# The end of even attention: one gated group finished apart, a bias as a product, and the heads first into the output projection

## The chip, the cores and the metric

The kernel runs on one core of one Trainium2 chip. The metric is the device time of one execution in microseconds (us); several runs are taken and their median is compared. The engines are named as in the profile: PE (matrix products), PEld (its weight loads), DVE (vector), ACT (activations and copies), POOL (a second elementwise engine), SP (which issues the DMAs).

## The reference

Two layers, each a mixer and a feed-forward network, over 512 tokens and 256 context tokens with 1024 channels, in fp32. The change lies in the mixer of the even layer. Its input projection gives u and v for a gated MLP over chunks of 128 tokens, and q, k and values for four heads of differential attention; both results, side by side, go through one output projection.

```python
def chunk_mlp(u, v, w_s, b_s):             # 4 groups of 128 channels
    u = gelu(u).reshape(shp)               # shp = (b, t // 128, 128, 4, 128)
    vf = gelu(v).reshape(shp)
    mu = mean(vf, axis=-1)
    vf = (vf - mu) * rsqrt(mean((vf - mu)**2, axis=-1) + EPS)
    mixed = einsum('gpq,bnqgc->bnpgc', w_s, vf) + b_s.T[None, None, :, :, None]
    return (u * mixed).reshape(b, t, A_WIDTH)

def diff_out(o, g, lam_init):              # o: attention's result by head
    return (rmsnorm(o, g) * (1.0 - lam_init)).reshape(b, t, B_V_WIDTH)

# even mixer, and the same for the context tokens with hc:
y = concatenate([chunk_mlp(u, v, w_s, b_s), diff_out(o, subln_g, lam_init)], -1) @ w_out
```

## The kernel before, in words

Activations lie with 128 channels on the partitions and all 768 tokens (512 and 256 context) along the row, so a tile of 128x768 is one group of channels. An fp32 product is made of three products of fp32r halves: `split` gives a tile's high half by a cast on ACT (L115) and its low half by a subtraction on DVE or POOL (L116), and `mm3` issues high by high (L99), high by low (L100) and low by high (L101). Weights are loaded by SP into a ring (`unit`, tile raw), cast on ACT (L75) and their low half is made on POOL (L78); the result is called w.

A tile framework sets the order of the instructions of each engine when the program is built, by the order in which they are written, by priorities, and by `issue_after`, which keeps an instruction behind a named one in that order and adds no wait of its own. The engines then run their queues in that order, each instruction waiting for its operands and for its buffers. PSUM has three short buffers (`bank`, tiles pb), one fill buffer (`fill`, tiles pf) and two wide ones (`wide`, pw).

The end of the even mixer's attention consists of these steps:

- `head(t)`: attention of a head, in three blocks of 256 queries. Its result o is normed by `norm`: squares on ACT (L592), sums over the channels on PE (L150), on DVE the mean (L159) and a root by three Newton steps (L129 to L133) on 128x6 numbers, six diagonal tiles q (L166), a product that spreads them over the partitions (L176), and the multiplication (L600). The root is written as one instruction for a start value and nine for the steps.
- `gated(i)`: 24 products of 512 and 24 of 256 columns into the fill buffer, copied to a tile f on ACT (L576). Groups 4 to 7 are v, groups 0 to 3 are u.
- `turn(g)`: group g of v is turned by PE (L635), copied back on ACT (L636), and its mean and variance are taken on DVE (L639, L640).
- then one `rstd_small` for all 24 columns of the four groups, and for each g `mix(g)`: normalising on DVE (L649), product with the chunk matrix sguT on PE (L650), the bias sgub added on DVE from a tile in which it is repeated on all partitions (L651).
- the cat loop: for u's groups the gelu on ACT (L623) and the gate product on DVE (L678), for all eight tiles the split into halves (tiles ax). The low halves of heads 5 and 6 are made on POOL.
- `project(half, ...)`: the output projection with the slabs of `even_out`, in the order of the list `order`, in two halves of the tokens, 192 products of 384 columns each. Between the casts of slabs on ACT stands the silu of the next stage's modulation with its table load (L206).

The two lines on which the ring's work depends are

```python
nc.scalar.copy(hi, raw)                                   # L75
eng.tensor_tensor(lo, raw, hi.bitcast(F32), ALU.subtract) # L78
```

## Time and profile before

| what | value |
|---|---|
| median of 3 runs | 1641.04 us (1639.45 to 1643.92) |
| profiled execution | 1640.6 us, its span 1638.8 us, mean granted clock 0.979 |
| PE busy | 1539.0 us, 94% of the span |
| DVE, ACT, POOL busy | 1098.8, 724.7, 650.6 us |
| chain that ended last | PE 79%, DVE 10%, ACT 4% |

The stretch that the change rewrites begins at 303.97 us of the span, with the first product of gated group 2, and its last part, the first half of the output projection, ends at 379.85. Rows of the timeline give the start, the duration, the engine, the line, the operation, out<-in and, in brackets, the idle time of that engine ahead of it with what ended it; "x8" are eight instructions in a row of one kind. The share of PEclk is the TensorE clock that the chip granted, 1.00 being full speed.

### The profile page before, as it was taken

To read this page: it belongs to the slowest core of one execution; us is meant where nothing else is said; L and a number is where in the kernel's file an instruction comes from. 1 tells how busy PE (TensorE), PEld (TensorE's weight loads), DVE (VectorE), ACT (ScalarE), POOL (GpSimd) and SP (SyncE) were. 2 spreads that over 40 slices of the span, in tenths; PEclk is the share of its full clock that TensorE was granted. 3 is DMA by queue.
4 is the path that set the end of the run, shared out by engine and by line. 5 is a ranking of instruction groups with operands and counts; after the bars stand their busy time and mean duration, and the time that the engine had idled before them with its cause. 6 is when DMAs were issued, how large, how long until landed. Compare 5 with 4: busy or idle time off the path is not lost.

```text
span 1638.8 us, 24612 instructions
## 1 busy us (share of the span) xinstructions
PE 1539.0 (94%) x9463; PEld 1352.8 (83%) x9463; DVE 1098.8 (67%) x2097; ACT 724.7 (44%) x1464; POOL 650.6 (40%) x477
## 2 busy tenths in 40 slices
PE   6999989989889999999999999999998799999997
PEld 4776777889678988999999978776867699999996
DVE  4621787755786888766667485675667876676565
ACT  2423675543452333333333344465555545444443
POOL 0563111050573334343333415531304665554563
PEclk9999989999999999999999999999999799999999
DMA  8744100123132234434432102100213232332311
GB/s 318 299 164 158 40 7 1 47 83 129 39 116 90 97 136 137 146 130 153 136 122 77 63 26 78 60 32 14 71 72 110 78 129 85 109 116 78 116 40 52
DMA packets 47957, 161.97 MB, mean 99 GB/s; under 512 B 5472, under 2 KB 9952, under 8 KB 40160
## 3 DMA queue, kind: packets, MB, share of 16 engines
q1 hardware_dynamic: 47696, 160.28, 28.0%
q8 instruction: 74, 1.21, 0.3%
q14 instruction: 43, 0.35, 0.1%
q10 hardware_dynamic: 144, 0.13, 0.1%
HBM read 158.29 MB, written 2.10 MB: 98 GB/s over the span
## 4 chain that ended last, share of the span: by engine, by line
PE 79%; DVE 10%; ACT 4%; issue 3%; POOL 2%; DMA 1%; SPq 0%; POOLq 0%; DVEq 0%; ACTq 0%
PE pw L99 10%; PE pw L100 10%; PE pw L101 10%; PE pb L100 9%; PE pb L101 9%; PE pb L99 9%; PE pf L99 3%; PE pf L100 3%; PE pf L101 3%; PE pb L1199 2%; PE pb L1193 2%; PE pf L350 2%; PE pw L1157 1%; PE pw L1165 1%; DVE hh L874 1%
## 5 line engine op out<-in xcount | busy, mean ns | idle before, releaser
L904 POOL TENSOR_TENSOR w<-raw,w 128x512 fp32r<-128x512 f32 x126 | 184.2, 1470 | 141.5 <-ACT w L902 132.7
L78 POOL TENSOR_TENSOR w<-raw,w 128x512 fp32r<-128x512 f32 (+1 forms) x84 | 125.7, 1504 | 232.6 <-ACT w L75 207.4
L99 PE MATMUL pw<-ax,w 128*128 128x384 f32 (+2 forms) x640 | 206.1, 326 | 6.7 <-ACT hs L969 4.1
L100 PE MATMUL pw<-ax,w 128*128 128x384 f32 (+2 forms) x640 | 207.8, 325 | 2.4 <-DVE ax L457 1.4
L101 PE MATMUL pw<-ax,w 128*128 128x384 f32 (+2 forms) x640 | 205.5, 324 | 0.0
L904 POOL TENSOR_TENSOR w<-rawo,w 128x512 fp32r<-128x512 f32 x80 | 114.1, 1427 | 214.7 <-ACT w L902 205.6
L758 DVE SCALAR_TENSOR_TENSOR xT<-pb,mod,xT 128x512 f32<-128x512 f32 (+3 forms) x208 | 144.9, 705 | 66.0 <-PE pb L101 65.4
L100 PE MATMUL pb<-hh,w 128*128 128x512 f32 x480 | 170.9, 358 | 1.9 <-POOL hh L116 1.9
L99 PE MATMUL pw<-T,w 128*128 128x384 f32 (+1 forms) x504 | 158.5, 317 | 13.0 <-ACT T L115 6.6
L902 ACT CAST w<-pf 128x512 fp32r<-128x512 f32 x152 | 89.4, 588 | 181.4 <-DVE pf L926 59.7
L101 PE MATMUL pb<-hh,w 128*128 128x512 f32 x480 | 168.6, 358 | 0.0
L99 PE MATMUL pb<-hh,w 128*128 128x512 f32 x480 | 164.9, 358 | 3.8 <-ACT hh L115 3.8
L100 PE MATMUL pw<-T,w 128*128 128x384 f32 (+1 forms) x504 | 158.5, 315 | 3.7 <-POOL T L116 2.4
L101 PE MATMUL pw<-T,w 128*128 128x384 f32 (+1 forms) x504 | 157.9, 313 | 0.0
L99 PEld LDWEIGHTS pw<-ax,w 128*128 128x128 f32 x640 | 122.8, 193 | 16.0 <-ACT hs L969 6.1
L904 DVE TENSOR_TENSOR w<-pf,w 128x512 fp32r<-128x512 f32 x152 | 104.2, 686 | 41.6 <-ACT w L902 37.5
L100 PEld LDWEIGHTS pw<-ax,w 128*128 128x128 f32 x640 | 123.3, 193 | 10.2 <-DVE ax L194 2.6
L101 PEld LDWEIGHTS pw<-ax,w 128*128 128x128 f32 x640 | 123.4, 193 | 3.4 <-POOL w L904 0.2
L99 PEld LDWEIGHTS pw<-T,w 128*128 128x128 f32 x504 | 97.0, 193 | 18.9 <-ACT T L115 8.6
L99 PE MATMUL pb<-ax,w 128*128 128x256 f32 (+1 forms) x340 | 104.0, 308 | 2.8 <-ACT w L75 1.6
L902 ACT CAST w<-raw 128x512 fp32r<-128x512 f32 x126 | 76.6, 622 | 63.8 <-PE pw L101 62.2
L100 PE MATMUL pb<-ax,w 128*128 128x256 f32 (+1 forms) x340 | 103.9, 306 | 1.0 <-DVE ax L116 0.9
(398 smaller groups left out, 4041.1 us busy)
## 6 DMA issues: line engine op xcount, KB each, us to landing
raw<-ffn_in SPq DMA_DIRECT2D x44, 1024.0 KB, 6.2
ar<-ada SPq DMA_DIRECT2D x24, 1024.0 KB, 7.1
ar<-ada SPq DMA_DIRECT2D x48, 512.0 KB, 3.5
rawo<-ffn_out SPq DMA_DIRECT2D x44, 512.0 KB, 3.8
raw<-odd_out SPq DMA_DIRECT2D x32, 256.0 KB, 2.7
raw<-qk SPq DMA_DIRECT2D x16, 256.0 KB, 7.9
raw<-uv SPq DMA_DIRECT2D x16, 256.0 KB, 2.8
raw<-even_out SPq DMA_DIRECT2D x8, 512.0 KB, 3.7
```

The costliest lines, as they stand in the source:

```text
L78: eng.tensor_tensor(lo, raw, hi.bitcast(F32), ALU.subtract)
L99: mm(out, s[0], m[0], start=start, stop=False, **kw)
L100: mm(out, s[0], m[1], start=False, stop=False, **kw)
L101: mm(out, s[1], m[0], start=False, stop=stop, **kw)
L350: nc.tensor.matmul(ps[32 * q:32 * q + 32, :w], cst[:, k, :], t[:, w * q:w * q + w], start=k == 0, stop=k == KT - 1, skip_group_check=True)
L758: self.nc.vector.scalar_tensor_tensor(h, ps[:, r], self.modcol(l, j, m, who), h, ALU.mult, ALU.add)
L874: sub = lambda out, x, y, how: nc.vector.tensor_tensor(out, x, y, how)
L902: nc.scalar.copy(t[:, 0, :], src)
L904: (eng or nc.gpsimd).tensor_tensor(t[:, 1, :], src, t[:, 0, :].bitcast(F32), ALU.subtract)
L1157: nc.tensor.matmul(ps[:, st:en], Q, K[g][p][:, b0 * P:b1 * P], start=p == 0, stop=p == 1, skip_group_check=True)
L1193: nc.tensor.transpose(pt[:, x * P:(x + 1) * P], es[2 * (x % 2) + x // 2][:, kb * P:(kb + 1) * P], self.ident)
L1199: nc.tensor.matmul(po[64 * h:64 * h + 64, :], V[vb][:, 64 * g:64 * g + 64], t[:, h * TC:h * TC + TC], start=kb == 0, stop=kb == nb - 1, sk ...
```

## The change

It has four parts.

- The root of v's variance is taken in two pieces, `finish(0, 3)` for 18 columns behind `gated(2)`, and `finish(3, 4)` for the last 6 behind the last head's diagonals. Each piece does its gelu and its mixing; mixing of groups 0 to 2 uses the fill buffer, that of group 3 the short ones.
- The bias is a product of two rows: ones2 (2x128) by brow, which holds the high and the low half of sgub. It starts the PSUM sum to which the mixing products add. The gate product then reads u and that sum, in two pieces per group.
- The fifth product step of `gated(3)` is ordered behind the last norm's sums.
- The four heads come first in `order`, and all low halves of the cat tiles are made on DVE.

```diff
@@ rstd_diag
-                nc.tensor.matmul(ps[:, c], acc[:, c], self.ones, start=j == 0, stop=not more, skip_group_check=True)
+                self.last_sum = nc.tensor.matmul(ps[:, c], acc[:, c], self.ones, start=j == 0, stop=not more,
+                                                 skip_group_check=True)
@@ loads
-            sgub = self.load(Rv, a["sgub"].partition_broadcast(P), [P, 512], "sgub")
+            brow = Rv.tile([2, 512], F32R, name="brow")
+            sgub = self.tmp("t")[0:2, :]
+            nc.sync.dma_start(sgub, a["sgub"].partition_broadcast(2))
@@ gated
-                self.dense(ps, W, A)
+                for k in range(KT):
+                    with tc.issue_after(self.last_sum.ins) if i == 3 and off == 0 and k == 4 else ExitStack():
+                        self.mm3(ps, W[k], A[k], k == 0, k == KT - 1)
@@ mix, finish
-        def mix(g, rs):
+        ones2 = Rv.tile([2, P], F32R, name="ones2")
+        nc.vector.tensor_copy(ones2, self.ones[0:2, :])
+        bhi = self.tmp()[0:2, :].bitcast(F32R)
+        nc.scalar.copy(bhi, sgub)
+        nc.vector.tensor_tensor(brow, sgub, bhi.bitcast(F32), ALU.subtract)
+        nc.scalar.copy(brow[0:1, :], bhi[0:1, :].bitcast(F32))
+
+        def mix(g, rs, o, bank):
...
-                pw = self.fill()
+                pw = bank()
+                nc.tensor.matmul(pw[:, :n * P].rearrange("p (n q) -> p n q", q=P), ones2,
+                                 brow[:, g * P:(g + 1) * P].unsqueeze(1).to_broadcast([2, n, P]), start=True, stop=False,
+                                 skip_group_check=True)
...
-                nc.vector.tensor_tensor(vg[...], pw[...], sgub[...], ALU.add)
+                nc.vector.tensor_tensor(raw[g][:, c], raw[g][:, c], pw[:, :n * P], ALU.mult)
+
+        def finish(g0, g1, bank):
+
+            rs = self.rstd_small(mv[:, 6 * g0:6 * g1, 1], 6 * (g1 - g0), 1.0, "sf")
+            for g in range(g0, g1):
+                self.last_gelu = gelu(g, self.last_exp)
+                mix(g, rs, 6 * g0, bank)
@@ even mixer, its end
         for g in range(4):
             turn(g)
             gated(g)
-        rs = self.rstd_small(mv[:, :, 1], 24, 1.0, "sf")
-        for g in range(4):
-            mix(g, rs)
+            if g == 2:
+                finish(0, 3, self.fill)
+        with tc.issue_after(self.last_diag.ins):
+            finish(3, 4, self.bank)
+        lastg = self.last_gelu
         cat = {}
-        order = [4, 5, 6, 0, 1, 2, 3, 7]
+        order = [4, 5, 6, 7, 0, 1, 2, 3]
         for k in order:
-            if k < 4:
-                lastg = gelu(k, self.last_exp)
-                nc.vector.tensor_tensor(raw[k], raw[k], raw[4 + k], ALU.mult)
-            src = raw[k] if k < 4 else oraw[k - 4]
             cat[k] = self.ax()
-            self.split(*cat[k], src, nc.gpsimd if k in (5, 6) else nc.vector)
+            self.split(*cat[k], raw[k] if k < 4 else oraw[k - 4])
```

Lines shift in the changed kernel: the transposes are L640, the statistics L644 and L645, the normalising L664, the mixing product L666, the bias product L659, the gate product L669, the diagonals L167, the spread L177, gated's copy L581, the gelu L628, the silu L207. In the rows below, out<-in are the program's names with the number of the tile.

On PE, ahead of gated group 3 (the first L99 row here is its first product; the sums L150, the transposes L640 and the spread L177 belong to the last head's norm and to group 3 of v), the changed kernel has:

```order
L666 MATMUL pf_3082<-sguT_1295,f_361_1980 128x128 x2
L659 MATMUL pf_3090<-brow,ones_1320 128x512
L666 MATMUL pf_3090<-sguT_1295,f_368_2043 128x128 x4
L150 MATMUL pb_2746<-ones,sq_2743 128x128 x4
L150 MATMUL pb_2752<-ones,sq_2743 128x128 x2
L659 MATMUL pf_3101<-brow,ones_1320 128x256
L666 MATMUL pf_3101<-sguT_1295,f_368_2043 128x128 x2
L640 MATMUL pf_3108<-ident_97,f_375_2106 128x128 x4
L640 MATMUL pf_3122<-ident_97,f_375_2106 128x128 x2
L177 MATMUL pb_2776<-q_2768,ones 128x512
L177 MATMUL pb_2779<-q_2773,ones 128x256
L99 MATMUL pf_3141<-ax_308,w_3132 128x512
```

Here one row is left out ahead of the last one (the bias product of group 3). Before, the transposes and the statistics of all groups stood ahead of gated 3, the norm's sums in its middle, and the mixing products and the spread behind it:

```order
L650 MATMUL pf_3129<-sguT_1295,f_353_1910 128x128 x4
L650 MATMUL pf_3139<-sguT_1295,f_353_1910 128x128 x2
L650 MATMUL pf_3145<-sguT_1295,f_360_1973 128x128 x4
L99 MATMUL pw_3312<-ax_3193,w_3256 128x384
L100 MATMUL pw_3312<-ax_3194,w_3256 128x384
L99 MATMUL pw_3313<-ax_3193,w_3256 128x384
L100 MATMUL pw_3313<-ax_3194,w_3256 128x384
L176 MATMUL pb_2769<-q_2761,ones 128x512
L176 MATMUL pb_2772<-q_2766,ones 128x256
```

Mixing of groups 0 to 2, the norm and group 3's transposes moved from behind or inside gated 3 to ahead of it; behind gated 3's last product (f is filled from pf_3167) stands at once the projection's first, L99 pw with w_3281.

On DVE, the last head's norm in the changed kernel (sm and its pb are the root's numbers, pf_3108 is the first half of group 3's transposes, q are the diagonals) reads:

```order
L669 TENSOR_TENSOR f_573_2984<-f_573_2984,pf_3101 128x256
L132 TENSOR_TENSOR sm_2757<-sm_2757,pb_2752 128x6
L133 SCALAR_TENSOR_TENSOR pb_2752<-sm_2757,pb_2752 128x6
L131 SCALAR_TENSOR_TENSOR sm_2757<-sm_2745,pb_2752 128x6
L132 TENSOR_TENSOR sm_2757<-sm_2757,pb_2752 128x6
L133 SCALAR_TENSOR_TENSOR pb_2752<-sm_2757,pb_2752 128x6
L131 SCALAR_TENSOR_TENSOR sm_2757<-sm_2745,pb_2752 128x6
L132 TENSOR_TENSOR sm_2757<-sm_2757,pb_2752 128x6
L644 BN_STATS stats<-pf_3108 128x6 x3
L133 SCALAR_TENSOR_TENSOR sm_2756<-sm_2757,pb_2752 128x6
L644 BN_STATS stats<-pf_3108 128x6
L167 TENSOR_SCALAR q_2768<-ident_97,sm_2756 128x128 x4
```

One row, three aggregates (L645), is left out ahead of the last. Between the root's steps stand the last mixing product and group 3's statistics, where before the bias additions L651 and the whole gate product L678 stood.

On ACT at the end of gated 3 (o are the heads' results, f_581 and f_591 the tiles of u's group 3, w the weights of the output projection) before:

```order
L115 CAST ax_3201<-o_2156 128x768
L576 COPY f_581_3062<-pf_3089 128x256
L623 ACTIVATE f_581_3062<-f_581_3062 128x768
L75 CAST w_3256<-raw_3257 128x1024
L75 CAST w_3255<-raw_3261 128x1024
```

and in the changed kernel:

```order
L115 CAST ax_3234<-o_2163 128x768
L581 COPY f_591_3140<-pf_3167 128x256
L115 CAST ax_3238<-o_2463 128x768
L628 ACTIVATE f_591_3140<-f_591_3140 128x768
L115 CAST ax_3242<-f_555_2814 128x768
L75 CAST w_3281<-raw_3282 128x1024
L115 CAST ax_3246<-f_564_2899 128x768
L75 CAST w_3280<-raw_3286 128x1024
```

The casts of head 7 and of u's groups 0 and 1 came in between the copy of gated 3 and the casts of the first weights. On POOL the two low halves (L116) ahead of the weights' low halves are gone, and on SP the sixth to eighth slab of even_out stand behind the loads of xT and ctxT.

10 lines of the change are left out of this document (5 added, 5 removed).

## The prediction

> **What bounds the kernel now.** I read the engines' busy time first: PE works 1539.0 of 1638.8 us, so only a stretch in which it stands is worth a change. The waits of PE in the stretch that the change rewrites (from the first product of gated group 2 to the end of the first half of the output projection) come next, longest first, and the same stretch cut by what PE does. After the times of a stretch, the columns give its length, the busy time of PE, its weight loads, DVE, ACT and POOL (instructions in brackets), then the granted clock, the DMA share and GB/s.
>
> ```profile
> PE 1539.0 (94%) x9463; PEld 1352.8 (83%) x9463; DVE 1098.8 (67%) x2097; ACT 724.7 (44%) x1464; POOL 650.6 (40%) x477
> ```
>
> ```profile
> PE pb L176 <- DVE q L166: 3.8, 1, 3.8
> ```
>
> ```profile
> 303.97:379.85 75.88, 69.27 (x405) 63.66 (x404) 44.96 (x119) 30.58 (x43) 23.68 (x10) 0.96 0.33 113
> 303.97:320.90 16.93, 15.92 (x101) 13.41 (x100) 9.57 (x40) 8.72 (x16) 0.00 (x0) 1.00 0.00 0
> 320.90:330.83 9.93, 9.93 (x60) 8.74 (x60) 9.48 (x41) 4.11 (x6) 0.88 (x1) 1.00 0.78 266
> 330.83:340.17 9.34, 3.74 (x26) 3.04 (x25) 7.82 (x17) 5.98 (x7) 8.61 (x4) 0.91 0.16 56
> 340.17:345.12 4.95, 4.95 (x11) 3.74 (x12) 3.02 (x6) 4.07 (x5) 2.70 (x2) 0.50 0.32 106
> 345.12:379.85 34.73, 34.73 (x210) 34.73 (x210) 15.07 (x18) 7.71 (x10) 11.49 (x5) 1.00 0.42 141
> ```
>
> The reader is to see three things. Gated group 3 (second cut) runs without a gap, and so does the projection from 345.12 on. In the third cut PE stands for 9.34 - 3.74 = 5.6 us, 3.84 of them in one wait for the last head's norm. In the fourth it is busy all the time, but at half clock. So all that can be won here is the idle time, 75.88 - 69.27 = 6.61 us, and the loss to the clock, 4.95 / 2 = 2.48: together 9.09 us. The rows of the third cut say who holds PE: mixing's matmuls (L650) and DVE's bias additions (L651) take turns, and the gate product (L678) stands on DVE ahead of the norm's diagonals (L166).
>
> ```profile
> 334.46 1.16 PE L650 MATMUL pf<-sguT,f 128*128 128x128 f32 x8 [0.52 <-DVE f L651]
> 340.17 2.93 PE L176 MATMUL pb<-q,ones 128*128 128x512 f32 x4 [3.84 <-DVE q L166]
> ...
> 332.49 0.69 DVE L651 TENSOR_TENSOR f<-pf,sgub 128x512 f32<-128x512 f32 x1 [1.17 <-PE pf L650]
> 334.44 2.79 DVE L678 TENSOR_TENSOR f<-f,f 128x768 f32<-128x768 f32 x1
> 337.34 3.17 DVE L166 TENSOR_SCALAR q<-ident,sm 128x128 f32<-128x128 f32 x6
> ```
>
> The clock fell inside that gap. Windows of 3.41 us that end where the clock changes, here and at a second gap (464.68 on):
>
> ```profile
> 334.88:338.29 3.41, 1.44 (x11) 1.13 (x9) 3.38 (x3) 1.01 (x2) 3.41 (x2) 1.00 0.21 64
> 338.29:341.70 3.41, 1.53 (x2) 0.84 (x3) 3.41 (x8) 3.40 (x4) 1.15 (x1) 0.52 0.56 195
> 341.70:345.12 3.42, 3.42 (x10) 2.91 (x9) 1.50 (x3) 2.54 (x3) 2.70 (x2) 0.50 0.12 49
> 464.68:468.09 3.41, 2.00 (x12) 1.68 (x10) 3.41 (x4) 1.33 (x3) 3.41 (x3) 1.00 0.58 191
> 468.09:471.51 3.42, 0.58 (x3) 0.58 (x4) 3.42 (x6) 2.00 (x5) 2.38 (x3) 1.00 0.67 231
> 471.51:474.92 3.41, 3.41 (x13) 3.41 (x12) 3.23 (x4) 1.62 (x4) 2.57 (x2) 0.50 0.83 281
> ```
>
> After a window with 1.44 or 0.58 us of work the next is at half clock; after one with 2.00 it is not; and a window at half clock with 1.53 of work is followed by another.
>
> **The change, part by part.** Its durations come from these rows, beside those above:
>
> ```profile
> 321.21 0.39 PE L100 MATMUL pf<-ax,w 128*128 128x512 f32 x1
> 321.44 0.40 PE L101 MATMUL pf<-ax,w 128*128 128x512 f32 x1
> 326.47 1.50 PE L150 MATMUL pb<-ones,sq 128*128 128x128 f32 x12
> 327.73 0.36 PE L99 MATMUL pf<-ax,w 128*128 128x256 f32 x1
> 327.93 0.28 PE L100 MATMUL pf<-ax,w 128*128 128x256 f32 x1
> 328.05 0.28 PE L101 MATMUL pf<-ax,w 128*128 128x256 f32 x1
> ...
> 306.12 0.17 DVE L133 SCALAR_TENSOR_TENSOR pb<-sm,pb 128x6 f32<-128x6 f32 x1
> 306.32 0.16 DVE L131 SCALAR_TENSOR_TENSOR sm<-sm,pb 128x6 f32<-128x6 f32 x1
> 306.91 1.27 DVE L166 TENSOR_SCALAR q<-ident,sm 128x128 f32<-128x128 f32 x6
> 318.44 0.89 DVE L639 BATCH_NORM_STATS2 stats<-pf 128x6 f32<-128x128 f32 x4 [0.57 <-ACT f L636]
> 323.40 6.25 DVE L649 TENSOR_SCALAR f<-f,mv,sf 128x128 f32<-128x128 f32 x24
> ...
> 328.25 2.30 ACT L115 CAST ax<-o 128x768 fp32r<-128x768 f32 x3 [0.94 <-PE pf L100]
> 330.87 0.37 ACT L576 COPY f<-pf 128x256 f32<-128x256 f32 x1 [0.32 <-PE pf L101]
> 331.27 0.84 ACT L623 ACTIVATE f<-f 128x768 f32<-128x768 f32 x1
> 332.02 1.98 ACT L75 CAST w<-raw 128x1024 fp32r<-128x1024 f32 x2
> ...
> 329.95 4.14 POOL L116 TENSOR_TENSOR ax<-o,ax 128x768 fp32r<-128x768 f32 x2 [54.63 <-ACT ax L115]
> 334.05 5.40 POOL L78 TENSOR_TENSOR w<-raw,w 128x1024 fp32r<-128x1024 f32 x2
> ```
>
> *Removed.* If nothing took the place of the old waits, all 9.09 us would go. The order of the changed kernel says that something does. Its PE runs gated 2, then mixing 0 to 2 with the last attention's products between, the norm's sums, group 3's transposes, the norm's spread, and only then gated 3 and, straight behind it, the projection. So the old places are filled by gated 3's work, and each chain that used to be covered by it now lies open ahead of it or behind it.
>
> *Bias as a product.* Eight products stand on PE's path: four of 512 columns at 321.44 - 321.21 = 0.23 us and four of 256 at 328.05 - 327.93 = 0.12, together +1.4. No row has a product over two rows; bounds are the 128x128 step, (327.73 - 326.47) / 12 = 0.105 each or +0.84, and the full 1.4. [...] On DVE the gate product takes the place of the addition and reads PSUM, so the four L678 go (2.79 for the one at 334.44). PE gets from that only the old waits, which are counted already.
>
> *Mixing on one buffer.* Each part's sum sits in the one fill buffer, so the next part waits for DVE's product. With work of attention or of the norm's sums between, nothing shows; bare, the wait is that of the row at 334.46, 0.52. Of the turns ahead of the norm two are not covered, one of them by half: +0.2 and +0.55. The second half of gated 2 has less between it and ACT's copy than before: +0.2. Bounds: 0, and four turns at 0.52, 2.1.
>
> *The norm of the last head.* It now has no gated products over it. From the end of its sums, DVE does 11 steps of the root at 306.32 - 306.12 = 0.2 (2.2), the last mixing product (0.35, half of 0.69), four BN_STATS (0.85, the scheduler put them between), three aggregates (0.25) and four of six diagonals (0.85): 4.5 us. In that time PE has group 2's second part and six transposes, 0.12 + 8 x 0.105 = 0.96, and some 0.3 until their result is out; 4.5 - 1.3 = **+3.2** of standing, in three pieces: the transposes' turn, the second transposes (which wait for statistics that stand behind the root) and the spread. Bounds: 0.85 less (BN_STATS first) and 1.9 more (diagonals at 3.17, as they ran beside POOL at 337.34; POOL has nothing to do here now, so I take 1.27).
>
> *The end of gated 3.* Its last copy, L576, waits for PE's last matmul, and behind it on ACT stand: the copy (331.27 - 330.87 = 0.40), the cast of head 7 (2.30 / 3 = 0.77), the gelu (332.02 - 331.27 = 0.75), the cast of group 0 (0.77) and only then the cast of the first weights (1.98 / 2 = 0.99), on which the projection's first product waits: 0.04 + 3.68 = **+3.7**. Before, these casts ran at 332.02, under the wait for the norm, and none of it showed. The low halves of the first slabs (POOL, 2.7 each) follow the casts; two products of three don't need them, so I add 0.3, with bounds 0 and one slab's 2.7.
>
> *What costs nothing.* The split of the root gives DVE 12 more steps (2.4 us), for 18 and for 6 columns; with 18 of the 24 normalisings (6.25 x 18 / 24 = 4.7) they move under gated 2, where DVE was busy 9.57 of 16.93, and they delay only mixing, counted above. If that cover were short, mixing 0 starts later by the difference. Group 3's root, six normalisings and mixing lie under gated 3's 9.93 us. The two low halves that POOL loses (4.14) go to DVE at 0.95 each, also under gated 3, where DVE has lost 4.7 of its 9.48. The order that ties gated 3's fifth product to the norm's sums moves nothing, since the sums stand ahead of gated 3 anyhow. On SP the bias load shrinks to two rows and moves later, and slabs 6 to 8 are issued behind the loads of xT and ctxT: the projection takes 34.73 / 8 = 4.3 us a slab, so the sixth is due after 21 us, and the queue runs at a DMA share of 0.42.
>
> *Clock.* The 3.7 us gap gives one window at half clock: 3.41 / 2 = 1.7. The norm's chain has about 1.2 us of PE's work in 4.5, under the 1.44 of above, so the clock falls there too; about 1 us of that window is still idle: (3.41 - 1) / 2 = 1.2. Bounds: 0 and two windows each, 6.8.
>
> The sum: new waits 0.2 + 0.75 + 3.2 + 3.7 + 0.3 = 8.15, products 1.4, clock 2.9, together 12.45; less 9.09: **+3.4 us**. From 345 on PE was and is full, so this reaches the end unchanged. The profiled run took 1640.6 us (its span of 1638.8 and 1.8 around it), 0.44 under the median; 1640.6 + 3.4 = 1644.0.
>
> [...]
>
> **Rivals.** A is the sum: 1644.0. B: only the long gap trips the clock, 1644.0 - 1.2 = 1642.8. For it: the pieces are short, and a window may be cut so that it holds 2.00 us. Against: 1.2 of 4.5 is less than any window above that kept the clock.
>
> C, slower: the half-clock window after the long gap is followed by a second one, because the projection starts on weights that come late. While PE waits between slabs for POOL's low halves it does less than about 1.5 to 2 of 3.41 us, and as at 338.29 to 345.12 the slow state goes on: +1.7, and 0.5 of such waits, 1646.2. It decides when the first slow window holds under some 1.5 us of work. For it: the row at 338.29 did just this, and POOL's first low half ends 2.7 us after the cast. Against: two products of three go on without.
>
> D, faster: the chains are hidden after all. If attention's last products run beside the norm and ACT is ahead of PE at the end of gated 3, the 3.7, the 3.2 and both clock terms go: 1644.0 - 9.8 = 1634.2. Against it: ACT's queue has the copy of gated 3's own result ahead of the weights, so only another order could hide that.
>
> **How the numbers follow.** A 0.44, B 0.20, C 0.23, D 0.09, and 0.04 for what I don't see, half of it slower. What a measurement can tell from no change is 0.3%, 4.9 us: A and B lie within, C above 1645.96, D below 1636.1. So faster 0.09, same 0.66, slower 0.25. The range leaves out D and the slower tail: 1638.5 (the long gap hidden, 1644.0 - 5.4) to 1648.5 (C with POOL's 2.7 in place of 0.5).
>
> **What would show it.** Right: PE's longest wait in this stretch is the projection's first product on ACT's weight cast, 3 to 4.5 us; the spread's wait on L166's successor is under 1.5; the group-3 transposes wait about 1.8 for statistics; the granted clock has a slow window behind each. Wrong: no wait ahead of the projection, or a spread that still waits over 3 us, or full clock throughout; each takes its own term out of the sum.

## The result, and the profile after

The changed kernel takes 1651.47 us in the median of 5 runs (1647.88 to 1652.67), the kernel before beside it 1640.87 us (5 runs): a ratio of 1.0058, with an interval of 1.0047 to 1.0069. It is slower by 0.58%, outside the range of the prediction. The profiled execution took 1647.88 us, with a span of 1646.1; it was the fastest of the five. One execution of all those below, of the kernel rows128_slabs_first, took 4682.25 us at a granted clock of 0.317 and is left out of the ratios.

The stretch from gated group 2 to the end of the projection's first half takes 82.39 us; before it took 75.88. Cut as in the prediction (columns as there), with the two windows at half clock as the last rows:

```profile
305.80:388.19 82.39, 74.16 (x414) 64.98 (x412) 38.57 (x124) 29.59 (x42) 19.85 (x8) 0.96 0.35 128
305.80:330.84 25.04, 23.75 (x149) 19.39 (x147) 16.76 (x67) 9.15 (x16) 0.00 (x0) 1.00 0.20 61
330.84:337.66 6.82, 4.58 (x12) 2.02 (x12) 6.26 (x36) 0.96 (x2) 0.00 (x0) 0.75 0.42 165
337.66:347.98 10.32, 10.32 (x62) 9.03 (x61) 3.84 (x12) 2.89 (x4) 0.00 (x0) 1.00 0.01 2
347.98:351.74 3.76, 0.16 (x3) 0.00 (x1) 3.56 (x6) 3.57 (x6) 0.00 (x0) 0.94 0.00 0
351.74:388.19 36.45, 35.34 (x193) 34.54 (x193) 8.16 (x7) 13.02 (x15) 19.85 (x8) 0.96 0.58 216
334.24:337.65 3.41, 3.41 (x5) 1.30 (x5) 3.15 (x17) 0.00 (x0) 0.00 (x0) 0.50 0.01 5
351.31:354.72 3.41, 2.98 (x9) 2.98 (x10) 3.02 (x2) 3.39 (x5) 2.90 (x2) 0.50 0.00 0
```

Three quantities can be taken from such rows: the idle time of PE (length less busy), the loss to the clock (half of the busy time of the last two rows, an estimate from their granted clock of 0.50; products of 384 columns start 0.32 us apart in the last one and 0.17 us behind it), and the rest, which is PE's work at full clock. Before: 6.61 idle, 2.5 lost, 66.7 work. After: 8.23 idle, (3.41 + 2.98) / 2 = 3.2 lost, 74.16 - 3.2 = 71.0 work. So of the 6.5 us the smaller part is idle time (+1.6) and clock (+0.7); +4.2 us is work, for which the prediction had 1.4.

The idle time lies where the prediction put it. From the timeline of PE (start, duration, line, what ran, idle time ahead of it and what ended it): the norm's pieces in the first three rows, the projection's first product, and one slab in the projection.

```profile
330.84 0.66 PE L640 MATMUL pf<-ident,f 128*128 128x128 f32 x4 [0.51 <-DVE f L669]
333.26 0.41 PE L640 MATMUL pf<-ident,f 128*128 128x128 f32 x2 [1.76 <-DVE stats L644]
334.14 2.44 PE L177 MATMUL pb<-q,ones 128*128 128x512 f32 x3 [0.47 <-DVE q L167]
...
351.74 0.69 PE L99 MATMUL pw<-ax,w 128*128 128x384 f32 x1 [3.60 <-ACT w L75]
...
379.35 0.44 PE L99 MATMUL pw<-ax,w 128*128 128x384 f32 x1 [1.00 <-ACT w L75]
```

The last row was not forecast. ACT waits there for a slab of even_out from SP's queue; the timelines of ACT and of SP:

```profile
348.17 0.37 ACT L581 COPY f<-pf 128x256 f32<-128x256 f32 x1 [0.32 <-PE pf L101]
348.44 0.83 ACT L115 CAST ax<-o 128x768 fp32r<-128x768 f32 x1
349.17 0.85 ACT L628 ACTIVATE f<-f 128x768 f32<-128x768 f32 x1
349.92 0.82 ACT L115 CAST ax<-f 128x768 fp32r<-128x768 f32 x1
350.64 1.04 ACT L75 CAST w<-raw 128x1024 fp32r<-128x1024 f32 x1
...
371.21 1.05 ACT L75 CAST w<-raw 128x1024 fp32r<-128x1024 f32 x1 [8.99 <-DMA raw<-even_out]
378.25 1.04 ACT L75 CAST w<-raw 128x1024 fp32r<-128x1024 f32 x1 [5.99 <-DMA raw<-even_out]
```

```profile
357.80 2.08 SPq L42 DMA_DIRECT2D xT<-xT  x4
359.98 1.52 SPq L42 DMA_DIRECT2D ctxT<-ctxT  x3
361.60 1.01 SPq L72 DMA_DIRECT2D raw<-even_out  x1
...
364.92 1.69 SPq L816 DMA_DIRECT2D raw<-ffn_in  x2
367.72 1.08 SPq L72 DMA_DIRECT2D raw<-even_out  x2
```

The sixth slab is issued at 361.60, behind seven loads of xT and ctxT, and is cast at 371.21; the last two follow at 367.72. The wait of 1.00 us is for the seventh, which is cast at 378.25. From issue to landing a slab takes 6.4 us in the median, before 3.7.

### The profile page after: what moved, and what is told of

It is laid out like the page before. It is cut to its first block, busy times and chain, and to the rows that moved or that the text cites. A ratio compares the mean times of both kernels' runs of the same rounds, so it can differ in the third digit from the quotient of the medians.

```text
span 1646.1 us, 24653 instructions
## 1 busy us (share of the span) xinstructions
PE 1544.6 (94%) x9471; PEld 1355.2 (82%) x9471; DVE 1092.6 (66%) x2108; ACT 726.1 (44%) x1466; POOL 646.2 (39%) x475
## 4 chain that ended last, share of the span: by engine, by line
PE 77%; DVE 10%; ACT 4%; issue 3%; POOL 3%; DMA 2%; SPq 0%; POOLq 0%; ACTq 0%; DVEq 0%
PE pw L99 10%; PE pw L100 10%; PE pw L101 10%; PE pb L100 9%; PE pb L101 9%; PE pb L99 9%; PE pf L99 3%; PE pf L100 2%; PE pf L101 2%; PE pb L1220 2%; PE pb L1214 2%; PE pf L351 2%; POOL w L78 1%; PE pw L1178 1%; PE pw L536 1%
## 5 line engine op out<-in xcount | busy, mean ns | idle before, releaser
L99 PE MATMUL pw<-ax,w 128*128 128x384 f32 (+2 forms) x640 | 206.3, 326 | 11.3 <-ACT w L75 4.6
L99 PE MATMUL pw<-T,w 128*128 128x384 f32 (+1 forms) x504 | 158.7, 317 | 13.7 <-ACT T L115 7.6
L99 PE MATMUL pb<-hh,w 128*128 128x512 f32 x480 | 164.7, 357 | 3.8 <-ACT hh L115 3.8
L99 PEld LDWEIGHTS pw<-ax,w 128*128 128x128 f32 x640 | 122.4, 192 | 21.2 <-ACT hs L990 6.1
L99 PEld LDWEIGHTS pw<-T,w 128*128 128x128 f32 x504 | 97.3, 194 | 19.2 <-ACT T L115 9.4
L99 PE MATMUL pb<-ax,w 128*128 128x256 f32 (+1 forms) x340 | 104.9, 310 | 3.2 <-ACT w L75 1.9
```

The source lines that it names most:

```text
L99: mm(out, s[0], m[0], start=start, stop=False, **kw)
```

## The experiments

Three theories stood at the start. P (product, R in the expectations): the bias product, not its place, is what the prediction missed; two rows between products of 128 rows cost more than their columns. S (slabs): the slabs that SP now issues behind xT and ctxT come late. Against both: the open chains (norm, gap ahead of the projection) or the order of the heads (part 4) carry the loss, and the products only look longer. A second question came up on the way, what held the norm for 3.84 us in the kernel before; the runs from diagonals_first on are for it.

The profiles are compared over the stretch of above, from the first product of gated group 2 to the end of the projection's first half, which are the same instructions in every kernel. A cut at a fixed time would not do: over all the profiles of this document the stretch begins between 303.97 and 307.07 us, although the instructions of the 60 us ahead of it stand in the same order in all of them. Idle, lost and work are taken as above, in us; each number is of one execution, and the clock's windows fall differently in each:

| kernel | length | idle | lost to clock | work |
|---|---|---|---|---|
| before, first and second profile | 75.9, 75.9 | 6.6, 6.6 | 2.5, 2.6 | 66.7, 66.7 |
| changed, first and second profile | 82.4, 83.2 | 8.2, 9.0 | 3.2, 3.1 | 71.0, 71.0 |
| rows128 | 78.8 | 8.6 | 1.7 | 68.5 |
| no_bias | 79.5 | 7.3 | 5.8 | 66.4 |
| bias_on_dve_in_change | 79.3 | 7.7 | 4.6 | 67.0 |
| slabs_first | 80.7 | 7.1 | 3.2 | 70.4 |
| rows128_slabs_first | 78.4 | 7.1 | 3.4 | 67.9 |
| bias_product_alone | 74.8 | 3.9 | 0.0 | 70.9 |
| rows128_alone | 76.1 | 5.4 | 3.0 | 67.8 |

The work follows the bias. Without a product on PE it is 66.4 to 67.0 in seven profiles (diagonals_first, norm_first_1 and norm_first_2 of below among them), with a product over 128 rows 67.8 to 68.5 in five, over two rows 70.4 to 71.0 in six; the means are 66.7, 68.1 and 70.8. So 128 rows cost 1.4 us, the price that the prediction had worked out from the columns, and two rows 4.1. Two kernels stand apart, low_halves_dve and low_halves_dve_add_late, with 68.1 and 68.0 without a product; why is not shown.

**Both kernels again**, unchanged, under the labels change_again and before_again.

> The change once more, unaltered, on the chip of the three runs beside it, so that its median, its late slabs and its clock windows can be set beside theirs. If the 1651.5 us of its first five runs belong to it, 1649 to 1653; if they were that chip's, near the sum of the stretch's profile, 1640.9 + 8.3 = 1649 or under.

> The kernel before, unaltered, for a second profile of it. Theory: the half-clock window that all profiles but the first one of before show around 275 to 284 us is a matter of where the clock's windows of 3.41 us fall, and stands here too or not without any edit; the time is that of before, 1640.5 to 1641.5. Rival: it belongs to the edits, and this profile has full clock from 250 to 330 us again.

The changed kernel: 1650.24 us (6 runs), ratio 1.0050 (1.0036 to 1.0065). The kernel before: 1640.34 (8 runs), 0.9992 (0.9981 to 1.0002). In the second profile of the changed kernel the late slabs cost PE 1.8 us instead of 1.0. The means of the two profiles in the table differ by 82.8 - 75.9 = 6.9 us: work 4.2, idle time 2.0, clock 0.6. The medians differ by 10.6 and 9.9. The 3 to 4 us between are not found in the stretch, and where they come from stays open: behind it the profiles of the two kernels take the same (1257.9 and 1260.3 us, and 1259.0 twice), and ahead of it kernels with the change and without it are equally late (the stretch begins at 305.7 and 305.6 us in the mean of 9 and 11 profiles).

**rows128**: the bias product over 128 rows, of which all but two of brow are zero. In the profile of the change the product of two rows takes 0.43 us to the next start with 512 columns and 0.31 with 256, where the rows of the prediction have 0.23 and 0.12 for other products of those widths.

```diff
-            brow = Rv.tile([2, 512], F32R, name="brow")
+            brow = Rv.tile([P, 512], F32R, name="brow")
-        ones2 = Rv.tile([2, P], F32R, name="ones2")
-        nc.vector.tensor_copy(ones2, self.ones[0:2, :])
+        ones2 = Rv.tile([P, P], F32R, name="ones2")
+        nc.vector.tensor_copy(ones2, self.ones)
+        zb = self.tmp()
+        nc.vector.memset(zb, 0.0)
+        nc.vector.tensor_copy(brow, zb)
```

> The change, with the bias product spread over 128 rows: ones2 is 128x128 ones and brow 128x512 with zeros below its two rows, so every result is the same and only the row count of the eight L659 products differs. [...] Then the 512-column product falls to 0.23 to 0.31 here, and PE's work in the stretch falls by 1.7 to 3 us against the change. Rival K (kind): the price comes from the switch between fp32 and fp32r products, or from the repeated moving operand; then L659 stays at 0.43 and 0.31 and the work stays. Time by R about 1648 to 1650 beside the change's 1651.5, by K no change.

1644.95 us (12 runs), ratio 1.0022 (1.0012 to 1.0032). The same group 0 on PE's timeline, in the changed kernel and then in this one (product L659 and L662, mixing L666 and L669, ahead of them four transposes of the attention):

```profile
316.38 0.60 PE L558 MATMUL pb<-ident,e 128*128 128x128 f32 x4
316.92 0.50 PE L659 MATMUL pf<-brow,ones 2*128 2x512 f32 x1
317.34 1.16 PE L666 MATMUL pf<-sguT,f 128*128 128x128 f32 x8
318.26 0.36 PE L100 MATMUL pb<-atl,vhi 128*128 128x256 f32 x1
```

```profile
317.65 0.60 PE L558 MATMUL pb<-ident,e 128*128 128x128 f32 x4
318.01 0.48 PE L662 MATMUL pf<-brow,ones 128*128 128x512 f32 x1
318.32 1.05 PE L669 MATMUL pf<-sguT,f 128*128 128x128 f32 x8
319.13 0.36 PE L100 MATMUL pb<-atl,vhi 128*128 128x256 f32 x1
```

Starts tell the cost better than durations, which overlap (the transposes' 0.60 from 316.38 reaches past the next start, 316.92). From the transposes to the attention's next product it is 1.88 us with two rows and 1.48 with 128. The two-row product holds PE for 0.42 instead of 0.31, the mixing behind it takes 0.92 instead of 0.81, and the transposes ahead of it 0.54 instead of 0.36. So 0.4 us of this product hangs on the number of rows alone. Over the eight products the work fell by 2.4 us. P holds. The time fell by 5.3 and 6.5 us against the two medians of the change, more than the 1648 to 1650 that I had expected; the stretch is 3.6 and 4.3 us shorter, 1.5 of it by a window at half clock that did not come, and the rest stays open. The 5.1 us of waits for the weights' cast remain (3.6 and 1.5), so S is not touched by it.

Of the 0.4 us, 0.18 lie ahead of the product, 0.11 in it and 0.11 behind it. Why the number of rows matters is not shown by a run here; a drain, as a later expectation has it, was not seen, only this price.

**no_bias**: no product and no bias, its loads left out.

```diff
-                nc.tensor.matmul(pw[...], ones2, brow[...], start=True, stop=False, skip_group_check=True)
...
-                                     sguT[:, g * P:(g + 1) * P], start=False, stop=True, skip_group_check=True)
+                                     sguT[:, g * P:(g + 1) * P], start=True, stop=True)
```

> The change without the bias altogether (it leaves the addition of b_s out): no L659, the gate product reads mixing's products as they are; all else in the change stays. It gives the whole price of the bias as a product, with what its place in the chain costs. Theory R: PE's work in the stretch from gated 2 to the end of the projection's first half falls by about 4.2 us (8 products at some 0.55), to that of before, 66.7; time about 1647. The prediction's own term says 1.4 us. Rival S (slabs): the time lies elsewhere, in weights that come late, and the total moves by less than 2 us.

1645.06 us (8 runs), 1.0026 (1.0016 to 1.0036). Its work is that of the kernel before (66.4 and 66.7): all the added work is the product, 4.6 us against either profile of the change, or 0.6 a product where the prediction had 1.4 / 8 = 0.17. The time is not below that of rows128, though the work is 2.2 us less and the idle time 1.3: its profile lost 5.8 us to the clock instead of 1.7. Whether its other executions did so too isn't shown.

**bias_on_dve_in_change**: part 2 undone, the bias added on DVE and then the gate product, as before.

```diff
-                nc.vector.tensor_tensor(raw[g][:, c], raw[g][:, c], pw[:, :n * P], ALU.mult)
+                nc.vector.tensor_tensor(vg[:, c]..., pw[:, :n * P]..., sgub[...], ALU.add)
+                nc.vector.tensor_tensor(raw[g][:, c], raw[g][:, c], vg[:, c], ALU.mult)
```

> The change with its second part undone: no bias product, DVE adds the bias from a tile on all partitions and then makes the gate product, per half group. Theory: PE's work falls by 5 us to that of before; DVE does eight more additions (0.69 and 0.42), of which one of 0.35 to 0.4 lies in the norm's chain: 1645 to 1646, beside 1645.1 without any bias. Rival: the additions hold the fill buffer no longer than the product did, but DVE comes late for the norm, and the spread's wait grows by 1 to 2 us with its half-clock window: 1647 to 1649.

1645.97 us (6 runs), 1.0030 (1.0019 to 1.0041). The work goes back to 67.0; the 3.6 ahead of the projection and the norm's 1.8 stay. Without part 2 the change is still slower than before, and what its profile loses then is clock (4.6 us, 2.1 more than before) and idle time (7.7 us, 1.1 more) and not work.

**slabs_first**: all slabs of even_out ahead of xT and ctxT on SP.

```diff
+        with tc.issue_after(self.last_w.ins):
             self.hxs, hcs = [[self.load(pool, a[x][r, :]...) for r in rows] for pool, x, T in (...)]
```

> The change with the loads of xT and ctxT ordered behind the last slab of even_out on SP, as they stood before; engines' orders stay. Theory S: in the profile of the change the cast of the seventh slab waited 8.99 and that of the eighth 5.99 us for its DMA, and PE waited 1.00 us there; with the slabs first these waits shrink and the PE wait of 1.00 goes; the time falls by 1 to 4 us, more in the runs in which the loads collide. Rival: xT then comes late, and the additions of the residual wait, and nothing is won.

1647.04 us (5 runs), 1.0035 (1.0022 to 1.0048). On SP the last three slabs now stand ahead of xT, and ACT casts the sixth at 366.75 instead of 371.21 (SP, then ACT):

```profile
360.91 5.03 SPq L72 DMA_DIRECT2D raw<-even_out  x3
365.99 1.96 SPq L42 DMA_DIRECT2D xT<-xT  x4
```

```profile
366.75 1.05 ACT L75 CAST w<-raw 128x1024 fp32r<-128x1024 f32 x1 [5.33 <-DMA raw<-even_out]
```

(The expectation counts one too far: the casts that waited 8.99 and 5.99 us were those of the sixth and the seventh slab.) PE waits for the weights' cast once, 3.6 us; the wait in the projection is gone. S holds. The idle time is 1.1 and 1.9 us less than in the two profiles of the change, the stretch 1.7 and 2.5 us shorter, and the median 4.4 and 3.2 us lower; the difference stays open here too.

**rows128_slabs_first**: both edits.

> The change with the bias product over 128 rows and the slabs of even_out ahead of xT and ctxT. Theory: rows128 took the drain out (2.1 us of PE's work, 1645.0 us), slabs_first took the late slab out (1 us and what hangs on it, 1647.0 us), and the two don't overlap; together 1641 to 1644, which is what the prediction's sum would have been with its own prices (+3.4). Rival: the clock's windows eat one of the two, and the time stays at 1645.

1643.44 us (12 runs), 1.0014 (1.0005 to 1.0023). This is 2.1 us over the kernel before beside it (1641.3). With the product cheaper and the slabs on time the changed kernel takes what the prediction said of the whole change: its +3.4 lies within the interval, which is +0.8 to +3.8 us (and within that of rows128, +2.0 to +5.2). The waits of the norm and the gap of 3.6 are unchanged.

**pool_casts_slabs_first**: the first three slabs' casts on POOL, so that the gap ahead of the projection is not ACT's, with the slabs' order of above.

```diff
-        nc.scalar.copy(hi, raw)
+        hi_eng.tensor_copy(hi, raw) if hi_eng else nc.scalar.copy(hi, raw)
...
-            Ws[k] = self.blocks(a["even_out"][k * P:(k + 1) * P, :], t=slots.pop())
+            Ws[k] = self.blocks(a["even_out"][k * P:(k + 1) * P, :], t=slots.pop(), hi_eng=nc.gpsimd if n < 3 else None)
```

> The change with the slabs first, and the casts of the first three slabs made on POOL, which does nothing from 305 to 351 us in the profile of the change, instead of on ACT behind gated 3's copy, the cast of head 7, the gelu and the cast of group 0. Theory W: the wait of 3.60 us ahead of the projection goes and with it its half-clock window (1.5 us), and the low halves are ready in time: 5 us less than the slabs alone. Rival P: POOL's cast of 128x1024 takes long (its subtraction takes 2.7) or slows DVE while both run, and the norm's diagonals go from 1.2 to 3.2 us; then less than 2.5 us are won.

1651.71 us (5 runs), 1.0061 (1.0048 to 1.0074): the wait of 3.6 went, and a longer one came behind it. PE, then DVE:

```profile
353.15 0.66 PE L99 MATMUL pb<-ax,w 128*128 128x384 f32 x1 [4.92 <-DVE f L669]
```

```profile
345.00 7.41 DVE L116 TENSOR_TENSOR ax<-o,ax 128x768 fp32r<-128x768 f32 x4 [6.06 <-ACT ax L115]
352.33 1.00 DVE L669 TENSOR_TENSOR f<-f,pb 128x512 f32<-128x512 f32 x2
```

The short PSUM buffers hold group 3's mixing sums until the gate product, which on DVE comes behind four low halves, 7.41 us in all beside POOL's casts. Part of this wait is POOL's own: in the changed kernel, where POOL stands idle until 351.81, the same four low halves take 0.9 to 1.0 us each, and the last gate product of group 3 ends at 351.19 us, 0.55 ahead of the projection. So the gap is not only ACT's, since even there the last of these buffers came free at 351.19; how long they would have held the projection up, had ACT been ready, isn't shown.

**old_order_in_change**: part 4 undone.

```diff
-        order = [4, 5, 6, 7, 0, 1, 2, 3]
+        order = [4, 5, 6, 0, 1, 2, 3, 7]
-            self.split(*cat[k], raw[k] if k < 4 else oraw[k - 4])
+            self.split(*cat[k], raw[k] if k < 4 else oraw[k - 4], nc.gpsimd if k in (5, 6) else nc.vector)
```

> The change with its fourth part undone: order 4, 5, 6, 0, 1, 2, 3, 7 again and the low halves of heads 5 and 6 on POOL. Theory: the casts of the first slabs still stand on ACT behind gated 3's copy, a cast, the gelu and another cast, and on SP xT and ctxT still go ahead of the last slabs, so both waits stay and the time is that of the change, 1648 to 1652. Rival: the heads first are what made the wait of 3.60 us; then it shrinks to 2 or less and the time falls below 1647.

1649.53 us (5 runs), 1.0053 (1.0041 to 1.0065), by its interval the time of the change. The gap of 3.6 is the same. The order of the heads is not the cause.

**bias_product_alone** and **rows128_alone**: the kernel before with part 2 alone, with two rows and with 128. The gelu moves ahead of each group's mixing in both.

```diff
                 pw = self.fill()
+                nc.tensor.matmul(pw[...], ones2, brow[...], start=True, stop=False, skip_group_check=True)
...
-                nc.vector.tensor_tensor(vg[...], pw[...], sgub[...], ALU.add)
+                nc.vector.tensor_tensor(raw[g][:, c], raw[g][:, c], pw[:, :n * P], ALU.mult)
...
         for g in range(4):
+            lastg = gelu(g, self.last_exp)
             mix(g, rs)
```

> The kernel before with the second part of the change alone: the bias as a two-row product, the gate product merged (so each gelu stands ahead of its mixing), root, orders and low halves as before. Theory R: eight products add 3 to 4.5 us of PE's work, of which those that fall into PE's idle time ahead of the norm cost nothing; DVE loses 2.8 us ahead of the norm's diagonals, so the wait of 3.84 for the spread shrinks to about 1 to 2 and may keep the clock. Net -3 to +2 us. [...]

> The kernel before with the second part of the change alone, and the bias product over 128 rows. With two rows this part alone stood at 1641.0, level with before: its stretch had 4.15 us more of PE's work, 2.7 less idle time and no half-clock window. Theory: over 128 rows the work falls by 2.1 us (as between the change and rows128), and at least half of that shows: 1639 to 1640. Rival: the time saved ahead of the norm turns into wait for its diagonals, which DVE sets: 1641.

1641.03 us (11 runs), 1.0000 (0.9992 to 1.0009), and 1642.23 (11 runs), 1.0009 (1.0000 to 1.0018). In the old place the same 4.1 us of work cost nothing in time. The waits for the norm, with two rows and with 128:

```profile
PE pb L176 <- DVE q L166: 1.6, 2, 1.4
```

```profile
PE pb L176 <- DVE q L166: 3.1, 1, 3.1
```

Only three of the eight products stand ahead of the norm (332.74 to 336.75 us with two rows), the other five between the products of the projection, where PE is full. There they show the price plainest; two rows, then 128:

```profile
349.34 0.34 PE L100 MATMUL pw<-ax,w 128*128 128x384 f32 x1
349.61 0.50 PE L656 MATMUL pf<-brow,ones 2*128 2x512 f32 x1
350.04 0.82 PE L662 MATMUL pf<-sguT,f 128*128 128x128 f32 x5
```

```profile
352.85 0.34 PE L100 MATMUL pw<-ax,w 128*128 128x384 f32 x1
353.02 0.39 PE L659 MATMUL pf<-brow,ones 128*128 128x512 f32 x1
353.25 1.05 PE L665 MATMUL pf<-sguT,f 128*128 128x128 f32 x8
```

From start to start the product takes 0.43 us with two rows and 0.23 with 128, which is the prediction's row for 512 columns, and the instruction ahead of it 0.27 and 0.17. What paid for the dear product in its profile is idle time, 2.7 us less than before, most of it the wait for the norm, and the clock, of which the stretch lost nothing (2.5 us before). With 128 rows 1.1 us of work came in, 1.2 us of idle time went and the clock's loss stayed. So the same product cost nothing where a wait and a half-clock window went with it, and 4 us under the change, where it shortened no such wait. That a dear product as such keeps the clock up isn't shown by one profile of each.

**no_split_rows128**: the kernel before with part 2 over 128 rows and with part 4, so without the split root and the reordered step (diffs as in rows128_alone, and the order of the heads as in the change).

> The change with its first and third part undone (one root for all 24 columns behind gated 3, as before) and the bias product over 128 rows; heads first and low halves on DVE stay. SP has all slabs ahead of xT again, and gated 3 lies over the root. Theory: what the change lost lies in the split, which moved mixing and the norm ahead of gated 3; without it no wait of 3.6 us stands ahead of the projection, and the time is 1638 to 1641. Rival: heads first put head 7, whose norm is the last thing ready, fourth in the projection, and PE waits for its spread and split: 1642 to 1645.

1646.79 us (6 runs), 1.0035 (1.0023 to 1.0047). I had thought that this would give the best version, 1638 to 1641, and it is slower than rows128_alone by 4.6 us:

```profile
PE pb L176 <- DVE q L166: 3.7, 2, 3.5
```

Without parts 1 and 3 the wait for the norm stands again, so it is these parts that remove it; what replaces it costs as much. The six diagonals take 7.62 us there, from 337.90, while POOL makes low halves of the weights from 335.64 to 345.44 with one break of 0.34: DVE meets POOL there too, though the low halves of heads 5 and 6 are on DVE. In the profiles the stretch of the two kernels differs by only 0.9 us (77.0 and 76.1); where the rest of the 4.6 comes from stays open.

**diagonals_first**: the kernel before with the gate products behind the last diagonals. The prediction had read the 3.84 us wait of before as the gate product's (L678), which stood ahead of the diagonals on DVE.

```diff
-                nc.vector.tensor_tensor(raw[k], raw[k], raw[4 + k], ALU.mult)
+                with tc.issue_after(self.last_diag.ins):
+                    nc.vector.tensor_tensor(raw[k], raw[k], raw[4 + k], ALU.mult)
```

> The kernel before with one line: the gate products L678 are ordered behind the last norm's diagonals on DVE, so that the 2.79 us product no longer stands ahead of them. Theory: the wait of 3.84 us for the spread shrinks by 2.8 to 4, and if a window then holds over 1.5 to 2 us of work the half clock (2.5 us) goes too: 1635 to 1638. Rival: the first group's cat tile comes 3 us later and the projection waits for it; or the clock falls all the same: 1639 to 1641.

1641.79 us (12 runs), 1.0005 (0.9996 to 1.0013): the wait is 2.9 us and the time the same. The gate product, 2.79 us in its old place, takes 0.95 behind the diagonals. On DVE the diagonals now take 4.91 us, and they end at 342.6, within 1 us of where POOL is done with the weights' low halves (DVE, then POOL):

```profile
337.75 4.91 DVE L166 TENSOR_SCALAR q<-ident,sm 128x128 f32<-128x128 f32 x6
```

```profile
332.99 4.18 POOL L116 TENSOR_TENSOR ax<-o,ax 128x768 fp32r<-128x768 f32 x2 [56.23 <-ACT ax L115]
337.13 4.67 POOL L78 TENSOR_TENSOR w<-raw,w 128x1024 fp32r<-128x1024 f32 x2
```

**norm_first_1, norm_first_2, norm_first_rows128**: as diagonals_first, with the mixing of groups 1 to 3, or of 2 and 3, behind the diagonals too, so that the norm comes earlier on DVE; the last with the bias product over 128 rows.

```diff
         for g in range(4):
-            mix(g, rs)
+            with tc.issue_after(self.last_diag.ins) if g >= 2 else ExitStack():
+                mix(g, rs)
```

> The same with the mixing of groups 1 to 3 behind the diagonals. Theory: the spread needs no wait at all, the second mixing product now waits for its normalising instead, covered by the spread and by the projection's first products: 1636 to 1639, level with norm_first_2 or a little below. Rival: PE waits for group 1's normalising where it waited for the diagonals: as before.

> The kernel before with the mixing of groups 2 and 3 and all gate products ordered behind the last norm's diagonals; root, bias, orders and gated 3 as before. On DVE the norm then waits for 12 normalisings instead of 24. Theory: the diagonals are done about 3.1 us earlier than in diagonals_first, whose wait for them was 2.9 us, so the wait for the spread falls under 1 us and the half-clock window goes: 1636 to 1639. Rival: the diagonals run beside POOL's low halves of heads 5 and 6 and take 3.2 us, or mixing comes late in turn, and the time stays within 1.5 us of before.

> norm_first_2 with the bias as a product over 128 rows and the merged gate product. PE's work grows by about 2 to 2.9 us, DVE's falls by four gate products, none of which stands ahead of the diagonals any more. Theory: with the wait gone there is nothing for the product to fill, so its work shows: 1 to 3 us above norm_first_2. Rival: DVE's lighter load brings the cat tiles forward and the product is free: level with norm_first_2.

1642.89 us (11 runs), 1.0008 (0.9999 to 1.0017); 1642.34 (11 runs), 1.0002 (0.9993 to 1.0011); 1643.83 (11 runs), 1.0014 (1.0005 to 1.0024). None reached the 1636 to 1639 that I had expected of the first two, and the bias product came to 1.5 us on top. In norm_first_2 DVE reached the diagonals at 331.85, 5.5 us earlier than before, and PE waited longer (5.84): six instructions took 7.46 us. DVE, then POOL:

```profile
331.85 7.46 DVE L166 TENSOR_SCALAR q<-ident,sm 128x128 f32<-128x128 f32 x6
```

```profile
330.63 3.60 POOL L116 TENSOR_TENSOR ax<-o,ax 128x768 fp32r<-128x768 f32 x2 [56.20 <-ACT ax L115]
334.17 4.67 POOL L78 TENSOR_TENSOR w<-raw,w 128x1024 fp32r<-128x1024 f32 x2
```

POOL's four low halves follow each other without a break and end at 338.84; the diagonals end at 339.31. Taken singly, the diagonals start at 331.85, 332.46, 334.23, 336.54, 338.84 and 339.04, and POOL's four instructions end at 332.46, 334.23, 336.53 and 338.84: as each of POOL's ends, one diagonal gets through. The earlier DVE is there, the longer it stands. So the wait was POOL's, not the gate product's. The next two runs test that from the other side.

**low_halves_dve, low_halves_dve_add_late**: the kernel before with all low halves of the cat tiles on DVE, behind the diagonals, so that POOL has nothing to do ahead of the first weights. The first also keeps the mixing of groups 2 and 3 behind the diagonals (norm_first_2), the second only the gate products and the bias additions.

```diff
-            self.split(*cat[k], src, nc.gpsimd if k in (5, 6) else nc.vector)
+            hi, lo = cat[k]
+            nc.scalar.copy(hi, src)
+            with tc.issue_after(self.last_diag.ins):
+                nc.vector.tensor_tensor(lo, src, hi.bitcast(F32), ALU.subtract)
```

> norm_first_2 with the low halves of all cat tiles on DVE, behind the last diagonals; POOL has then only the weights' low halves, the first of which waits for its cast on ACT (about 335 us). Theory P (POOL holds DVE): the six diagonals take 1.2 to 1.4 us instead of 7.46, the spread's wait of 5.84 falls to under 0.5, and PE waits some 1.5 us for the first cast instead: PE's idle time in the stretch falls by 3 to 4 us and the half-clock window may go: 1636 to 1639. Rival D (DVE's own work ahead of the diagonals): their duration stays over 3 us and the time at 1641 to 1642.

> diagonals_first with the low halves on DVE and with mixing's bias additions too behind the diagonals; all 24 normalisings stay ahead of them. Theory P: the diagonals start near 332 and end near 333, before or just as POOL starts on the first slab; they take 1.3 to 2 us, the wait for the spread falls to 0.5 to 1.5 us; but the low half of head 4 then runs beside POOL (2.3 instead of 0.95) and PE waits for it some 1 to 2 us: 1637 to 1640. Rival D: 1641 to 1642.

1641.22 us (12 runs), 0.9995 (0.9985 to 1.0005), and 1639.59 (10 runs), 0.9981 (0.9971 to 0.9990). The first, of which I had expected 1636 to 1639, is level with before. The second beats both kernels: 0.19% under the kernel before and, by the two ratios to that kernel, 0.8% under the change. It is the best of sixteen variants, so some of the 0.19% may be luck. In it, DVE, POOL and PE around the norm:

```profile
332.70 1.26 DVE L166 TENSOR_SCALAR q<-ident,sm 128x128 f32<-128x128 f32 x6
...
334.49 5.87 DVE L686 TENSOR_TENSOR ax<-o,ax 128x768 fp32r<-128x768 f32 x2
```

```profile
334.08 5.46 POOL L78 TENSOR_TENSOR w<-raw,w 128x1024 fp32r<-128x1024 f32 x2 [59.54 <-DVE q L166]
```

```profile
333.63 1.12 PE L176 MATMUL pb<-q,ones 128*128 128x512 f32 x2 [0.29 <-DVE q L166]
```

With POOL idle the six diagonals take 1.26 us, the spread waits 0.29, and no window of this stretch is at half clock (1.00 granted from 304.86 to 379.74). Of the 6.6 + 2.5 us that the prediction counted as the most to be won, the clock's 2.5 is gone in this profile. That it is what the medians differ by (2.4) isn't shown: the stretch is 1.0 us shorter than before (74.9), and that of low_halves_dve, where the products of 384 columns between 341 and 350 start the 0.17 us of full clock apart and the six diagonals take 1.27 us, is 2.3 us shorter (73.6) without a gain in time. The idle time stays, 6.9 us in the stretch, since the low halves on DVE now meet POOL's (5.87 us for two) and PE waits for them instead:

```profile
PE pw L100 <- DVE ax L686: 2.9, 3, 1.2
PE pb L99 <- DVE o L600: 1.6, 1, 1.6
```

So the six diagonals took 1.26 and 1.27 us with POOL idle, and 4.91 and 7.46 beside it, in norm_first_2 with one diagonal at the end of each of POOL's four instructions. Two subtractions on DVE took 5.87 us beside POOL, and 0.90 and 0.96 each in the changed kernel with POOL idle. How POOL holds DVE is not shown.

## Why the prediction was wrong, step by step

Its sum was +3.4, and the stretch gave +6.5 in the first profile and +7.2 in the second. By its terms:

| term | forecast | first profile |
|---|---|---|
| old waits and clock removed | -9.09 | -9.15 |
| mixing on one buffer | 0.95 | 0.78 |
| norm of the last head | 3.2 | 0.51 + 1.76 + 0.47 = 2.74 |
| gap at the end of gated 3 | 3.7 | 3.60 |
| waits inside the projection | 0.3 | 1.11 |
| clock | 2.9 | 3.2 |
| bias as a product | 1.4 | 4.2 |

With +6.5 in place of +3.4 the sum would have been 1647.1 us, inside the range. That the median came to 1651.47 needs the 3 to 4 us besides that no profile here places.

**What held.** The reading of the order: each chain that gated group 3 had covered lies open, in the places named, for the times named. The gap of 3.60 is the five ACT instructions of the rows above, added up from their rows of before. Both windows at half clock came, so rival B fell: no piece of the norm's chain was over 1.76, and the window from 334.24 was at half clock all the same. The window ahead of it, from 330.83, held 1.16 us of work, under the 1.44 that the prediction had read. What B counted on, a window's edge that cuts the pieces, came in rows128: 1.89 and 2.19 us of work in the windows from 328.62 and 332.04, and the clock stayed (1.00 granted from 326 to 340). These edges are an estimate: a granted clock of 0.69 from 347.8 to 351.3 puts the start of the half-clock window behind the gap at 349.1, and they lie six and five steps of 3.41 us, the length of the half-clock windows above, ahead of it. Rival D needed another order and had none.

**What failed: the price of the bias product.** The forecast took the columns for the whole price, 1.4 us. For two rows that was my estimate: no row of before had a product over two rows, no run shows that price for them, and the bound that I gave above it was the same 1.4, so that the range had no room. Measured: 4.2 us, 0.5 us each. For 128 rows the columns were priced rightly: over them the eight products add 1.4 us (68.1 of work against 66.7). With two rows they add 2.7 us more (70.8), 0.3 each, in the product itself and in the instruction ahead of it. Taken away, the product leaves the work of before (no_bias). The sum expected of rows128_slabs_first has 2.1 us for a drain that goes with 128 rows; no run shows a drain, and what the profiles show in its place is PE's work, 71.0 us with two rows and 68.5 with 128, and 70.4 and 67.9 with the slabs first.

**What failed: "what costs nothing" on SP.** I set the sixth slab's due time, 21 us into the projection, against a DMA share of 0.42, which is a mean over the stretch. The queue's order says more: the fifth slab waits for a buffer until 357.42, and behind it seven loads go out in a row, ahead of the sixth. The sixth was still in time; the seventh, due 4.3 us later, was not, and cost PE 1.0 and 1.8 us in the two profiles, where the term had 0. slabs_first takes that away. Rival C gave a time near this one by late weights, but by another way: PE's first window behind the gap was followed by one at full clock (1.00 from 354.72 to 358.13), and POOL's low halves didn't hold it up (none of PE's waits from 303 to 390 us is for POOL).

**What was misread and did not matter to the sum.** The 3.84 us wait of before was put on the gate product ahead of the diagonals. It was POOL's low halves that held DVE, in the diagonals, as the prediction saw, and in the gate product too: 2.79 us where it takes 0.95 elsewhere, and 3.17 where the diagonals take 1.27, are 3.7 us too long together. With the gate product out of the way the wait stood (2.9), with POOL out of the way as well it went (0.29). In the changed kernel POOL does nothing around the norm (0.00 us in 330.84 to 337.66 above). Had I seen that, the forecast would have been the same, but a better change would have been in sight.

In the stretch the change is slower because it trades 9 us of waits and clock for about 11 of them, and adds 4.2 us of products in a place where they shorten no wait. (The ends of the prediction's range are 1638.6 and 1648.4 by its own sums; nothing hangs on the 0.1.)

## What to carry to other kernels

An operation that no row of the trace shows gets a bound that is worse than its columns, above all if it differs in kind from its neighbours: the product of two rows took 0.43 us where 512 columns had taken 0.23. The added products were free in bias_product_alone (1.0000), where 2.7 us of idle time and the half clock went with them, and cost 4 us under the change, where they shortened no such wait; so ask whether the same change takes that wait away. Before a wait is put on the instruction ahead in the queue, compare the duration of the waited-for instruction with its duration elsewhere: six diagonals at 3.17 us, and 1.27 in another place, were the sign here that another engine held them, and with POOL idle they took 1.26. When loads are reordered, count what stands ahead of each on its queue and when that is issued, not the mean share of the DMA engines.

## What was not expected of the hardware

A product of two rows between products of 128 rows cost 0.3 us more than the same with 128 in the mean of eight (70.8 and 68.1 us of work in all), and 0.4 in the group shown (1.88 and 1.48 us), of which the product's own time is 0.11, the one ahead 0.18 and the ones behind 0.11. DVE's six 128x128 fp32 diagonals did not slow down beside POOL's subtractions by a fixed factor: they took 1.26 us with POOL idle (low_halves_dve_add_late), 4.91 beside it in diagonals_first and 7.46 in norm_first_2, where they came earlier (331.85 against 337.75) and got through one at a time as a POOL instruction ended. And in the changed kernel the TensorE clock fell to 0.50 in the window from 334.24, after idle pieces of 0.51, 1.76 and 0.47 us within 3.8; with pieces of 0.52, 1.76 and 0.47 it stayed at 1.00 in rows128, where by the estimate above they lay across the edge of two windows. The 1.7 us that the stretch of rows128 lost to the clock are one window, the one behind the gap.
